# An encoder block on one core: value products of two heads side by side, low halves of seven weights made on DVE, and 20 instead of 16 k-tiles of the down projection in seven products

## Chip, core and metric

One core of one Trainium2 chip. The metric is the device time of one execution in microseconds (us). Of the kernel before there are three timed executions; one further execution was profiled.

## What is computed

One encoder block on 512 tokens of 1024 channels, batch 1, in float32. Two mixers work side by side on the normalised input, attention with 8 query heads and 2 key/value heads of 64, and a Mamba-2 state space model in both directions; gates merge them, an output projection and a residual follow, and then a SwiGLU feed-forward layer of width 2816.

```python
h = rms_norm(x, norm1_pre)
q, k, v, z, xbc, dt_raw, gates = split_cols(h @ w_in, IN_SPLITS)
attn_out = gqa_attention(rope(rms_norm(q)), rope(rms_norm(k)), v) @ w_attn_proj
ssd_out = ssd_branch(z, xbc, dt_raw, ...) @ w_ssd_proj
g_attn, g_ssd = split(sigmoid(gates), 2)
x = x + rms_norm((g_attn * attn_out + g_ssd * ssd_out) @ w_out, norm1_post)
gate, up = split(rms_norm(x, norm2_pre) @ w_gate_up, 2)
x = x + rms_norm((silu(gate) * up) @ w_down, norm2_post)
```

## The kernel before

**High and low halves.** To keep float32 accuracy, each operand of a large matmul is split in a high half (`whi`, a cast on ACT, L144) and a low half (`wlo`, the operand less its high half), and each product is three matmuls (`mm3`, L178 to L180, and `mm3f`, L1125). `weights()` lists the weights in the order of their use with a letter that says who makes the low half. "v" and "g" are a subtract on DVE or on POOL (L149). "d" is a negation on ACT (L146) and a DMA, issued by POOL, that reads the weight a second time and adds it in flight (L147). `presplit` carries this out, up to `AHEAD` weights before the use.

**Attention.** For each head the scores are made (L635, L636), a softmax follows, and `transpose_probs` turns the probabilities on PE (L653) with copies to SBUF by DVE and ACT. For each pair of heads eight value products of 64 columns of weights follow (L677): for each of four key tiles one product for either head, the one into the lower half of a PSUM bank, the other into the upper. A tile scheduler orders the instructions of this part; the z and gate products fill in between.

**Feed-forward.** `act` holds 22 k-tiles of 128 channels by 512 tokens. From the output projection on, PE's order is that of the program; the other engines' is the scheduler's.

**Down projection** (`down_start`, `down`). The output has four token tiles and two halves of 512 columns, in eight PSUM banks. The first 6 k-tiles are plain: 24 matmuls of 512 columns each. The other 16 (`PAIRS` = 8 pairs) are one 2 by 2 block product with a fast scheme of seven products: tokens split in halves `lo` and `hi`, k-tiles in two halves, columns in two halves. A pair of k-tiles takes 42 matmuls so. The seven products (into `u`, `v`, `a`, `x`, `u`, `a`, `y`) are each cut in groups of two k-tiles (`NG2` = 4 groups). `prep(g)` makes the high and low halves of a group's weights (`wsplit`, L1195 on ACT, L1196 on DVE) and activations (`asplit`, L1201, L1202), and `work(g)` issues the matmuls; `prep` stands one group ahead. Sums of blocks of weights are formed in `chain` (`ch`): once a group has been split, a DMA issued by POOL adds the next block into it (L1225). A second buffer `p3` holds the sum that the fourth product needs. Sums of activations are made by DVE behind the groups (`sums`, L1312 and L1313).

**Tail.** `begin(t)` squares the second column half of token tile `t` and multiplies it by the gain; `finish(t)` does so with the first half, makes the reciprocal root and writes the output with the residual (L1270). In the last product `last(2)` and `last(3)` do the sum and `finish` of the last two token tiles.

Of the kernel before, what the change touches and what calls it, by code (L numbers as in the profile page):

```python
# [14 lines left out]
ALU = mybir.AluOpType  # L15
# [4 lines left out]
P = 128  # L20
# [5 lines left out]
NQ = 8  # L26
# [18 lines left out]
PAIRS = 8  # L45
# [15 lines left out]
class Block:  # L61
# [41 lines left out]
    def weights(self):  # L103

        a = self.a
        for k0, kn in ((0, 3), (3, 3), (6, 2)):
            yield a["w_kv"][:, k0 : k0 + kn, :], kn * 288, "v" if k0 == 0 else "d"
        for j in range(12):
            yield a["w_xbc"][j], 1024, "g" if j < 3 else "d"
        for n in range(2):  # L110
            for i in range(4):
                yield a["w_z"][n, i], 1024, "gd"[n]
        for j in range(2 * KD):
            yield a["w_g"][j], 1024, "d"
# [533 lines left out]
    def transpose_probs(self, prs):  # L648
        pt = []
        for k in range(NT):  # L650
            pp = self.ps("sb")
            for t in range(NT):
                self.T.transpose(pp[:, t * P : t * P + P], prs[t][:, k * P : k * P + P], self.ident)  # L653
# [5 lines left out]
    def attention(self, decays):  # L659
# [3 lines left out]
        for h in range(NQ):  # L663
# [8 lines left out]
            if h % 2:  # L672
                po = self.ps("sc")
                for k in range(NT):
                    for i in range(2):
                        g = (h - 1 + i) // (NQ // NKV)
# [476 lines left out]
    def down(self, pool):  # L1153
# [7 lines left out]
        p3 = [new("p3", [2, 512], NG2) for _ in range(NG2)]  # L1161
# [9 lines left out]
        mm3, plain, bank = self.mm3f, self.plain, self.bank  # L1171

        for k in range(1, n0):
            if k > 1:
                self.down_operands(k, pool)
                if k < n0 - 2:
                    for t, n in bank:
                        plain(k, t, n)
            if k == 1:
                gain = [new("gn", [512], 2) for _ in range(2)]  # L1180
                for i in range(2):
                    self.load(gain[i], self.a["norm2_post"][i * 512 : i * 512 + 512].partition_broadcast(P))
            if k >= 2 and k - 2 < NG2:
                self.load(chain[k - 2], blk(k - 2, 0, 0))
        for t, n in reversed(bank):
            for k in (n0 - 2, n0 - 1):
                plain(k, t, n)
# [28 lines left out]
        def product(dst, b, a, start, after=None, sums=None, by_token=None, then=None):  # L1216
# [3 lines left out]
            def prep(g):  # L1220
# [3 lines left out]
                if after:  # L1224
                    G.dma_start(chain[g], after(g), accum_op=ALU.add)  # L1225

            def work(g):
                for k in (2 * g, 2 * g + 1):
                    x, wi = kept[k]
                    for t in range(1 if by_token else 2):  # L1230
                        mm3(dst[t], [y[:, t * P : t * P + P] for y in x], wi, start and k == 0)
                    if sums:
                        sums(k)
                if g == NG2 - 1:
                    if by_token:
                        by_token()
                        for x, wi in kept:
# [11 lines left out]
        def begin(t):  # L1249
# [5 lines left out]
            self.square_sum(ss[:, 0:1], c[t, 1], self.rstd[:, t : t + 1])  # L1255
            V.tensor_scalar(ss[:, 0:1], ss[:, 0:1], 1.0 / D, EPS, ALU.mult, ALU.add)
            V.tensor_tensor(c[t, 1], c[t, 1], gain[1], ALU.mult)
            half[t] = x, ss

        def finish(t):  # L1260
            x, ss = half[t]
            r2 = self.rstd[:, t : t + 1]
            self.square_sum(ss[:, 1:2], c[t, 0], r2)
            V.tensor_tensor(c[t, 0], c[t, 0], gain[0], ALU.mult)
# [4 lines left out]
            for i in (1, 0):  # L1269
# [8 lines left out]
        def third_weights():  # L1278
            for g in range(NG2):
                self.load(p3[g], blk(g, 0, 1))  # L1280
                G.dma_start(p3[g], blk(g, 1, 1), accum_op=ALU.add)
# [10 lines left out]

        def sums6():
            for t in range(2):
# [5 lines left out]
                begin(2 + t)  # L1300
# [5 lines left out]
        def last(t):  # L1306
            add(t, 0, y[t - 2])
            finish(t)

        between = {4: lambda: begin(0), 5: lambda: begin(1), 6: lambda: finish(0), 7: lambda: finish(1)}  # L1310
        product(u, lambda g: chain[g], a11, True, lambda g: blk(g, 0, 1),
                lambda k: V.tensor_tensor(r1[k], a22(k), a21(k), ALU.subtract), then=third_weights)  # L1312
        product(v, lambda g: raw(g, 1, 0), a12, False, None, lambda k: V.tensor_tensor(a21(k), a11(k), a21(k), ALU.subtract),  # L1313
                then=sums2)
        product(a, lambda g: chain[g], lambda k: r1[k], True, lambda g: blk(g, 1, 1),
                lambda k: V.scalar_tensor_tensor(r1[k], r1[k], -1.0, a11(k), ALU.mult, ALU.subtract), then=lambda: second(a))
        product(x, lambda g: p3[g], a21, True, None,
                lambda k: V.scalar_tensor_tensor(a12(k), r1[k], -1.0, a12(k), ALU.mult, ALU.subtract), then=lambda: second(x))
# [132 lines left out]
```

## Time and profile before

| what | us |
|---|---|
| three timed executions | 827.84, 830.14, 832.91 |
| median | 830.14 |
| profiled execution, own time | 830.12 |
| its span in the trace | 828.2 |
| mean granted clock of TensorE | 0.991 |

The profiled execution's time is 1.9 us longer than the span that the trace covers. In all views times count from the span's start. A row of the timeline gives start and duration of an instruction, or of several of one kind in a row (x2, x3). A duration includes the drain of the pipeline: of two instructions in a row the second starts before the end that is shown for the first. A piece of the chain of waits has start, length and what the time went to.

### The profile page before, as it was taken

Reading aid. Unit: us, or ns where it says so; the run is one execution under the profiler, and the core shown is the slowest. Engines: PE = TensorE matmul, PEld = TensorE weight load, DVE = VectorE, ACT = ScalarE, POOL = GpSimd, SP = SyncE. Lnnn points to the kernel's source line nnn. Section 1 sums busy time; section 2 is a strip of 40 time slices with the busy share of each in tenths; the row PEclk is TensorE's granted clock in tenths of the full one; section 3 lists DMA queues with packets and bytes.
Section 4 is the critical chain, followed back from the end, with each engine's and each line's share of the span. In section 5 each row is a group of like instructions: output and inputs, shape, how many; then the busy total and the mean of one; then the engine's idle time right before and its main releaser. Section 6 shows DMA issues by size and latency. Waiting matters only on the chain.

```text
span 828.2 us, 12209 instructions
## 1 busy us (share of the span) xinstructions
PE 804.9 (97%) x4522; PEld 676.8 (82%) x4522; DVE 578.4 (70%) x999; ACT 465.8 (56%) x841; POOL 200.0 (24%) x162
## 2 busy tenths in 40 slices
PE   8899999999899999999999999999999999999994
PEld 7688887666676777777888798999999999888883
DVE  3959785656335456685783799788888878837988
ACT  7767875745844442166333656555555555536673
POOL 3443430100132244539451002000000100041200
PEclk9999999999999999999999999999999999999998
DMA  9757830620875665137335453667766664899642
GB/s 314 218 134 159 200 93 27 140 64 1 216 176 130 158 150 124 52 114 252 116 129 185 164 153 91 188 193 188 193 177 185 182 178 140 286 288 245 104 93 102
DMA packets 49658, 130.52 MB, mean 158 GB/s; under 512 B 5568, under 2 KB 5952, under 8 KB 49600
## 3 DMA queue, kind: packets, MB, share of 16 engines
q1 hardware_dynamic: 38048, 95.46, 33.7%
q0 software_dynamic: 11552, 34.30, 24.0%
q8 instruction: 35, 0.57, 0.3%
q14 instruction: 23, 0.19, 0.1%
HBM read 121.35 MB, written 8.39 MB: 157 GB/s over the span
## 4 chain that ended last, share of the span: by engine, by line
PE 83%; DVE 5%; DMA 4%; ACT 3%; issue 2%; POOL 1%; SPq 1%; DVEq 0%; ACTq 0%; POOLq 0%
PE sa L972 10%; PE mm L178 8%; PE mm L179 8%; PE mm L180 8%; PE sc L972 7%; PE sb L1125 4%; PE sa L1125 4%; PE mm L972 3%; PE sb L972 3%; PE mm L1125 3%; PE sc L178 3%; PE sc L180 3%; PE sc L179 3%; PE sc L677 2%; PE sa L179 2%
## 5 line engine op out<-in xcount | busy, mean ns | idle before, releaser
L144 ACT CAST whi<-raw 128x1024 fp32r<-128x1024 f32 (+3 forms) x69 | 68.0, 992 | 20.6 <-PE sc L180 9.8
L178 PE MATMUL mm<-hT,wlo 128*128 128x512 f32 x176 | 73.8, 419 | 2.1 <-DMA wlo<-in_w_g 2.1
L149 POOL TENSOR_TENSOR wlo<-raw,whi 128x1024 fp32r<-128x1024 f32 (+1 forms) x28 | 58.2, 2081 | 65.5 <-ACT whi L144 63.9
L180 PE MATMUL mm<-hT,whi 128*128 128x512 f32 x176 | 69.7, 396 | 0.0
L179 PE MATMUL mm<-hT,whi 128*128 128x512 f32 x176 | 69.3, 394 | 0.0
L1023 POOL DMA_DIRECT2D raw<-in_w_gu x19 | 16.4, 861 | 211.5 <-ACT x L1114 54.8
L1028 ACT CAST whi<-raw 128x512 fp32r<-128x512 f32 (+1 forms) x57 | 41.6, 762 | 33.9 <-DMA raw<-in_w_gu 12.9
L1029 DVE TENSOR_TENSOR wlo<-raw,whi 128x512 fp32r<-128x512 f32 (+1 forms) x57 | 47.8, 866 | 16.3 <-ACT whi L1028 16.3
L972 PE MATMUL sa<-R,whi 128*128 128x256 f32 x304 | 56.4, 283 | 0.0
L972 PEld LDWEIGHTS sa<-R,whi 128*128 128x128 f32 x304 | 47.5, 192 | 0.0
L146 ACT ACTIVATE wlo<-raw 128x1024 fp32r<-128x1024 f32 (+2 forms) x31 | 32.3, 1043 | 26.4 <-PE mm L178 24.4
L972 PE MATMUL sa<-R,wlo 128*128 128x256 f32 x152 | 43.1, 283 | 0.0
L178 PEld LDWEIGHTS mm<-hT,wlo 128*128 128x128 f32 x176 | 33.3, 189 | 11.8 <-issue 3.2
L147 POOL DMA_DIRECT2D wlo<-in_w_g x16 | 13.8, 863 | 112.6 <-ACT wlo L146 66.7
L179 PEld LDWEIGHTS mm<-hT,whi 128*128 128x128 f32 x176 | 33.3, 189 | 8.7 <-issue 2.4
L180 PEld LDWEIGHTS mm<-hT,whi 128*128 128x128 f32 x176 | 33.3, 189 | 7.6 <-issue 0.5
L638 DVE TENSOR_REDUCE nmax<-sa 128x1 f32<-128x512 f32 x32 | 21.6, 686 | 19.9 <-PE sa L636 19.7
L972 PE MATMUL sa<-h2T,b 128*128 128x256 f32 x228 | 30.5, 283 | 0.0
L641 ACT ACTIVATE pr<-sa,nmax 128x512 f32<-128x512 f32 x32 | 22.0, 688 | 14.6 <-DVE rc L643 7.4
L972 PEld LDWEIGHTS sa<-R,wlo 128*128 128x128 f32 x152 | 29.2, 192 | 0.0
L155 ACT ACTIVATE junk<-z 128x512 bf16<-128x512 f32 x8 | 5.0, 628 | 42.6 <-DVE z L785 42.5
L972 PEld LDWEIGHTS sa<-h2T,b 128*128 128x128 f32 x228 | 28.7, 192 | 0.0
(475 smaller groups left out, 2552.8 us busy)
## 6 DMA issues: line engine op xcount, KB each, us to landing
raw<-in_w_gu SPq DMA_DIRECT2D x44, 512.0 KB, 4.7
raw<-in_w_gu POOLq DMA_DIRECT2D x19, 512.0 KB, 5.4
raw<-in_w_g SPq DMA_DIRECT2D x16, 512.0 KB, 6.0
wlo<-in_w_g POOLq DMA_DIRECT2D x16, 512.0 KB, 6.8
raw<-in_w_dn SPq DMA_DIRECT2D x14, 512.0 KB, 7.2
raw<-in_w_xbc SPq DMA_DIRECT2D x12, 512.0 KB, 4.9
ch<-in_w_dn POOLq DMA_DIRECT2D x12, 512.0 KB, 7.2
b<-in_w_gu SPq DMA_DIRECT2D x19, 256.0 KB, 5.8
```

The costliest lines, as they stand in the source:

```text
L144: self.A.copy(h[:, :n], raw[:, :n])
L146: self.A.mul(l[:, :n], raw[:, :n], -1.0)
L149: e.tensor_tensor(l[:, :n], raw[:, :n], h[:, :n].bitcast(F32), ALU.subtract)
L178: self.T.matmul(o, ll, rh, start=first, stop=False)
L179: self.T.matmul(o, lh, rl, start=False, stop=False)
L180: self.last_mm = self.T.matmul(o, lh, rh, start=False, stop=last)
L638: V.tensor_reduce(nmax, ps, AX.X, ALU.max, negate=True)
L641: self.last_exp = A.activation(pr, ps, AF.Exp, bias=nmax, accum_out=sm)
L972: self.T.matmul(dst, x, y[:, k], start=start and k == 0 and i == 0, stop=k == 3 and i == 2, skip_group_check=True)
L1028: A.copy(dst[0], src)
L1029: lo.tensor_tensor(dst[1], src, dst[0].bitcast(F32), ALU.subtract)
L1125: self.T.matmul(o, x, y, start=start and i == 0, stop=i == 2, skip_group_check=True)
```

## The change

Three parts. In `attention` the value products of a head pair are issued behind the last transpose of the second head, and listed as alternating heads. In `weights` the second key/value group, the second half of the z weights and the first two gate weights change their letter from "d" to "v". In `down` 20 of the 22 k-tiles go through the seven products (10 pairs, 5 groups), the two plain ones are those of `down_start`; `p3` goes. Instead blocks (0,0) and (0,1) are loaded into `b11` and `chain`. Behind a group's split in the first product POOL adds `chain` to `b11` (`first_sums`, L1275 of the changed program) and a DMA adds block (1,1) to `chain`; behind the fourth and fifth product further blocks are added to `chain`. The final normalisation can begin with either column half: token tiles 0 and 1 begin with half 0 behind the fourth product, 2 and 3 with half 1 behind the fifth, and 0 and 1 finish in the last product behind its k-tiles 8 and 9. Six of the eight gain products go to POOL. In the last product the first group serves both token tiles at once, and only the last four groups are split by token.

```diff
@@ -42,7 +42,7 @@
 R_DTB, R_AL, R_D, R_QK, R_END = 0, 32, 64, 80, 336
 
 
-PAIRS = 8
+PAIRS = 10
 NPLAIN = 3
 
 
@@ -104,14 +104,14 @@
 
         a = self.a
         for k0, kn in ((0, 3), (3, 3), (6, 2)):
-            yield a["w_kv"][:, k0 : k0 + kn, :], kn * 288, "v" if k0 == 0 else "d"
+            yield a["w_kv"][:, k0 : k0 + kn, :], kn * 288, "d" if k0 == 6 else "v"
         for j in range(12):
             yield a["w_xbc"][j], 1024, "g" if j < 3 else "d"
         for n in range(2):
             for i in range(4):
-                yield a["w_z"][n, i], 1024, "gd"[n]
+                yield a["w_z"][n, i], 1024, "gv"[n]
         for j in range(2 * KD):
-            yield a["w_g"][j], 1024, "d"
+            yield a["w_g"][j], 1024, "v" if j < 2 else "d"
         for j in range(KD):
             yield a["w_ap"][j], 512, "g"
         for j in range(KD):
@@ -650,7 +650,7 @@
         for k in range(NT):
             pp = self.ps("sb")
             for t in range(NT):
-                self.T.transpose(pp[:, t * P : t * P + P], prs[t][:, k * P : k * P + P], self.ident)
+                self.last_tr = self.T.transpose(pp[:, t * P : t * P + P], prs[t][:, k * P : k * P + P], self.ident)
             d = self.slot("t", [S], name="pt")
             (self.A.copy if k % 2 else self.V.tensor_copy)(d, pp)
             pt.append(d)
@@ -671,9 +671,10 @@
             yield 1.8
             if h % 2:
                 po = self.ps("sc")
-                for k in range(NT):
-                    for i in range(2):
-                        g = (h - 1 + i) // (NQ // NKV)
+
+                for k, i in ((k, i) for k in range(NT) for i in range(2)):
+                    g = (h - 1 + i) // (NQ // NKV)
+                    with self.tc.issue_after(self.last_tr.ins):
                         self.T.matmul(po[i * HD : i * HD + HD, :], self.vt[:, k, g * HD : g * HD + HD], pts[h - 1 + i][k],
                                       start=k == 0, stop=k == NT - 1)
                 hi, lo = self.slot("q", [S], F32R, "aTh"), self.slot("q", [S], F32R, "aTl")
@@ -1158,7 +1159,7 @@
         NG2 = PAIRS // 2
         new = lambda tag, shape, bufs, dt=F32: pool.tile([P] + shape, dt, tag=tag, name=self.nm(tag), bufs=bufs)
         chain = [new("ch", [2, 512], NG2) for _ in range(NG2)]
-        p3 = [new("p3", [2, 512], NG2) for _ in range(NG2)]
+        b11 = [new("b11", [2, 512], NG2) for _ in range(NG2)]
         r1 = [new("r1", [256], PAIRS) for _ in range(PAIRS)]
         splits = [new("as", [2, 256], 10, F32R) for _ in range(10)]
         cs = [new("c", [512], 8) for _ in range(8)]
@@ -1168,23 +1169,14 @@
             j = n0 + k * PAIRS + 2 * g
             return wd[j : j + 2, :, n * 512 : n * 512 + 512].rearrange("k p c -> p k c")
 
-        mm3, plain, bank = self.mm3f, self.plain, self.bank
-
-        for k in range(1, n0):
-            if k > 1:
-                self.down_operands(k, pool)
-                if k < n0 - 2:
-                    for t, n in bank:
-                        plain(k, t, n)
-            if k == 1:
-                gain = [new("gn", [512], 2) for _ in range(2)]
-                for i in range(2):
-                    self.load(gain[i], self.a["norm2_post"][i * 512 : i * 512 + 512].partition_broadcast(P))
-            if k >= 2 and k - 2 < NG2:
-                self.load(chain[k - 2], blk(k - 2, 0, 0))
-        for t, n in reversed(bank):
-            for k in (n0 - 2, n0 - 1):
-                plain(k, t, n)
+        mm3, bank = self.mm3f, self.bank
+
+        for g in range(NG2):
+            self.load(b11[g], blk(g, 0, 0))
+            self.load(chain[g], blk(g, 0, 1))
+        gain = [new("gn", [512], 2) for _ in range(2)]
+        for i in range(2):
+            self.load(gain[i], self.a["norm2_post"][i * 512 : i * 512 + 512].partition_broadcast(P))
         c = {(t, 1): cs.pop() for t in (2, 3, 0, 1)}
         for (t, n), x in c.items():
             A.copy(x, bank[t, n])
@@ -1222,19 +1214,19 @@
                 for i in range(2):
                     kept.append((asplit(a(2 * g + i)), [y[:, i * 512 : i * 512 + 512] for y in w]))
                 if after:
-                    G.dma_start(chain[g], after(g), accum_op=ALU.add)
+                    after(g)
 
             def work(g):
                 for k in (2 * g, 2 * g + 1):
                     x, wi = kept[k]
-                    for t in range(1 if by_token else 2):
+                    for t in range(1 if by_token and g >= NG2 - 4 else 2):
                         mm3(dst[t], [y[:, t * P : t * P + P] for y in x], wi, start and k == 0)
                     if sums:
                         sums(k)
                 if g == NG2 - 1:
                     if by_token:
                         by_token()
-                        for x, wi in kept:
+                        for x, wi in kept[2 * (NG2 - 4) :]:
                             mm3(dst[1], [y[:, P : 2 * P] for y in x], wi)
                     if then:
                         then()
@@ -1246,27 +1238,27 @@
 
         half = {}
 
-        def begin(t):
+        def begin(t, n):
 
             x = [new("x2", [512], 4) if t < 2 else self.slot("a", [512], name="x2") for _ in range(2)]
             for i in range(2):
                 self.load(x[i], self.x2_d[t][:, i * 512 : i * 512 + 512])
             ss = self.tiny(2, "ss")
-            self.square_sum(ss[:, 0:1], c[t, 1], self.rstd[:, t : t + 1])
+            self.square_sum(ss[:, 0:1], c[t, n], self.rstd[:, t : t + 1])
             V.tensor_scalar(ss[:, 0:1], ss[:, 0:1], 1.0 / D, EPS, ALU.mult, ALU.add)
-            V.tensor_tensor(c[t, 1], c[t, 1], gain[1], ALU.mult)
+            G.tensor_tensor(c[t, n], c[t, n], gain[n], ALU.mult)
             half[t] = x, ss
 
-        def finish(t):
+        def finish(t, n):
             x, ss = half[t]
             r2 = self.rstd[:, t : t + 1]
-            self.square_sum(ss[:, 1:2], c[t, 0], r2)
-            V.tensor_tensor(c[t, 0], c[t, 0], gain[0], ALU.mult)
+            self.square_sum(ss[:, 1:2], c[t, n], r2)
+            (G if t < 2 else V).tensor_tensor(c[t, n], c[t, n], gain[n], ALU.mult)
             v = self.tiny(1, "rv")
             V.tensor_scalar(v, ss[:, 1:2], 1.0 / D, ss[:, 0:1], ALU.mult, ALU.add)
             r = self.rsqrt(v, 1, True)
             V.tensor_tensor(r, r, r2, ALU.mult)
-            for i in (1, 0):
+            for i in (1 - n, n):
                 V.scalar_tensor_tensor(c[t, i], c[t, i], r, x[i], ALU.mult, ALU.add)
                 self.load(self.out[t * P : t * P + P, i * 512 : i * 512 + 512], c[t, i])
 
@@ -1275,10 +1267,13 @@
         x = [self.ps("sb") for _ in range(2)]
         v, y = [bank[t, 0] for t in (0, 1)], [bank[t, 0] for t in (2, 3)]
 
-        def third_weights():
-            for g in range(NG2):
-                self.load(p3[g], blk(g, 0, 1))
-                G.dma_start(p3[g], blk(g, 1, 1), accum_op=ALU.add)
+        def more(k, n):
+
+            return lambda g: G.dma_start(chain[g], blk(g, k, n), accum_op=ALU.add)
+
+        def first_sums(g):
+            G.tensor_tensor(b11[g], b11[g], chain[g], ALU.add)
+            more(1, 1)(g)
 
         def sums2():
             for t in range(2):
@@ -1289,6 +1284,11 @@
         def second(p):
             for t in range(2):
                 add(2 + t, 1, p[t], ALU.subtract)
+
+        def third():
+            second(x)
+            for t in range(2):
+                begin(t, 0)
 
         def sums6():
             for t in range(2):
@@ -1297,7 +1297,7 @@
                 add(2 + t, 1, u[t], ALU.subtract)
                 add(t, 1, u[t], ALU.subtract)
                 add(2 + t, 0, x[t])
-                begin(2 + t)
+                begin(2 + t, 1)
 
         def sums3():
             for t in range(2):
@@ -1305,18 +1305,18 @@
 
         def last(t):
             add(t, 0, y[t - 2])
-            finish(t)
-
-        between = {4: lambda: begin(0), 5: lambda: begin(1), 6: lambda: finish(0), 7: lambda: finish(1)}
-        product(u, lambda g: chain[g], a11, True, lambda g: blk(g, 0, 1),
-                lambda k: V.tensor_tensor(r1[k], a22(k), a21(k), ALU.subtract), then=third_weights)
+            finish(t, 0)
+
+        between = {8: lambda: finish(0, 1), 9: lambda: finish(1, 1)}
+        product(u, lambda g: b11[g], a11, True, first_sums,
+                lambda k: V.tensor_tensor(r1[k], a22(k), a21(k), ALU.subtract))
         product(v, lambda g: raw(g, 1, 0), a12, False, None, lambda k: V.tensor_tensor(a21(k), a11(k), a21(k), ALU.subtract),
                 then=sums2)
-        product(a, lambda g: chain[g], lambda k: r1[k], True, lambda g: blk(g, 1, 1),
+        product(a, lambda g: b11[g], lambda k: r1[k], True, None,
                 lambda k: V.scalar_tensor_tensor(r1[k], r1[k], -1.0, a11(k), ALU.mult, ALU.subtract), then=lambda: second(a))
-        product(x, lambda g: p3[g], a21, True, None,
-                lambda k: V.scalar_tensor_tensor(a12(k), r1[k], -1.0, a12(k), ALU.mult, ALU.subtract), then=lambda: second(x))
-        product(u, lambda g: chain[g], lambda k: r1[k], False, lambda g: blk(g, 1, 0), then=sums6)
+        product(x, lambda g: chain[g], a21, True, more(0, 0),
+                lambda k: V.scalar_tensor_tensor(a12(k), r1[k], -1.0, a12(k), ALU.mult, ALU.subtract), then=third)
+        product(u, lambda g: chain[g], lambda k: r1[k], False, more(1, 0), then=sums6)
         product(a, lambda g: raw(g, 1, 1), a12, False, then=sums3)
         product(y, lambda g: chain[g], a22, False, None, lambda k: between.get(k, int)(), lambda: last(2))
         stages[0][0]()
```

On PE, a pair of heads, before: `sb` is the bank of the second head's transposes, `sc` that of the value products, `pt` the turned probabilities, `mm` a z or gate product.

```order
L677 MATMUL sc_1618<-pt_1468,vt_448 64x512
L178 MATMUL mm_1605<-whi_1172,hT_344 128x512
L179 MATMUL mm_1605<-wlo_1173,hT_342 128x512
...
L653 MATMUL sb_1598<-cst_100,pr_1433 128x128
L653 MATMUL sb_1598<-cst_100,pr_1444 128x128
L677 MATMUL sc_1618<-pt_1582,vt_448 64x512
L677 MATMUL sc_1618<-pt_1475,vt_448 64x512
L677 MATMUL sc_1618<-pt_1589,vt_448 64x512
L677 MATMUL sc_1618<-pt_1482,vt_448 64x512
L677 MATMUL sc_1618<-pt_1596,vt_448 64x512
L677 MATMUL sc_1618<-pt_1489,vt_448 64x512
L677 MATMUL sc_1618<-pt_1603,vt_448 64x512
```

And now:

```order
L653 MATMUL sb_1597<-cst_100,pr_1421 128x128
L653 MATMUL sb_1597<-cst_100,pr_1432 128x128
L653 MATMUL sb_1597<-cst_100,pr_1443 128x128
L678 MATMUL sc_1617<-pt_1467,vt_447 64x512
L678 MATMUL sc_1617<-pt_1581,vt_447 64x512
L678 MATMUL sc_1617<-pt_1474,vt_447 64x512
L678 MATMUL sc_1617<-pt_1588,vt_447 64x512
L678 MATMUL sc_1617<-pt_1481,vt_447 64x512
L678 MATMUL sc_1617<-pt_1595,vt_447 64x512
L678 MATMUL sc_1617<-pt_1488,vt_447 64x512
L678 MATMUL sc_1617<-pt_1602,vt_447 64x512
L180 MATMUL mm_1604<-whi_1235,hT_342 128x512
```

The product that stood alone among the `mm` matmuls now stands with the other seven behind the transposes, in alternation of the heads.

On DVE, the key/value stage, before (`h` and `hT` are the normalised input and its low halves, `wlo` the low half of a key/value group):

```order
L149 TENSOR_TENSOR wlo_356<-raw_135,whi_355 128x864
L184 TENSOR_TENSOR hT_343<-h_351,hT_341 128x512
L184 TENSOR_TENSOR hT_343<-h_359,hT_341 128x512
L294 SCALAR_TENSOR_TENSOR h_368<-xT_110,gcol_99,rbs_349 128x512
L294 SCALAR_TENSOR_TENSOR h_372<-xT_115,gcol_99,rbs_349 128x512
L294 SCALAR_TENSOR_TENSOR h_381<-xT_120,gcol_99,rbs_349 128x512
L184 TENSOR_TENSOR hT_343<-h_368,hT_341 128x512
```

The same place now:

```order
L149 TENSOR_TENSOR wlo_356<-raw_135,whi_355 128x864
L184 TENSOR_TENSOR hT_343<-h_351,hT_341 128x512
L184 TENSOR_TENSOR hT_343<-h_359,hT_341 128x512
L149 TENSOR_TENSOR wlo_364<-raw_137,whi_363 128x864
L294 SCALAR_TENSOR_TENSOR h_367<-xT_110,gcol_99,rbs_349 128x512
L294 SCALAR_TENSOR_TENSOR h_371<-xT_115,gcol_99,rbs_349 128x512
L294 SCALAR_TENSOR_TENSOR h_380<-xT_120,gcol_99,rbs_349 128x512
```

A second subtract of 128 by 864 stands ahead of the `h` and `hT` of the later k-tiles.

On DVE, in the first product of the down projection, now (`as` is a split activation, `r` and `act` the sums of activations):

```order
L1312 TENSOR_TENSOR r_1526_7374<-act_6670,act_5330 128x256
L1312 TENSOR_TENSOR r_1527_7375<-act_4342,act_5464 128x256
L1188 TENSOR_TENSOR wlo_7423<-b_1517_7365,whi_7422 128x1024
L1194 TENSOR_TENSOR as_7388<-act_5866,as_7388 128x256
L1194 TENSOR_TENSOR as_7389<-act_6000,as_7389 128x256
L1312 TENSOR_TENSOR r_1528_7376<-act_4343,act_5598 128x256
L1312 TENSOR_TENSOR r_1529_7377<-act_4344,act_5732 128x256
L1312 TENSOR_TENSOR r_1530_7378<-act_4345,act_5866 128x256
L1312 TENSOR_TENSOR r_1531_7379<-act_4346,act_6000 128x256
L1188 TENSOR_TENSOR wlo_7433<-b_1518_7366,whi_7432 128x1024
L1313 TENSOR_TENSOR act_4737<-act_4737 128x256
L1313 TENSOR_TENSOR act_4928<-act_4928 128x256
```

and on POOL, from the last weight load of the layer ahead on:

```order
L1024 DMA raw_7130<-in_w_gu 128x1024
L1275 TENSOR_TENSOR b_1517_7365<-b_1517_7365,ch_7360 128x1024
L1272 DMA ch_7360<-in_w_dn 128x2x512
L1275 TENSOR_TENSOR b_1518_7366<-b_1518_7366,ch_7361 128x1024
L1272 DMA ch_7361<-in_w_dn 128x2x512
...
L1275 TENSOR_TENSOR b_1521_7369<-b_1521_7369,ch_7364 128x1024
L1272 DMA ch_7364<-in_w_dn 128x2x512
L1249 TENSOR_TENSOR c_7393<-c_7393,gn_7408 128x512
L1249 TENSOR_TENSOR c_7392<-c_7392,gn_7408 128x512
L1272 DMA ch_7360<-in_w_dn 128x2x512
```

Each subtract `wlo<-b` on DVE is now followed on POOL by a sum into the same `b` and a DMA into `ch`, and behind the fifth stand gain products (L1249). The sums and the gain products on POOL are new; DMAs into `ch` stood there before too.

## Rows read from the trace of the kernel before

**Rows 1.** The page, busy times of the engines (share of the span, instructions)

```profile
PE 804.9 (97%) x4522; PEld 676.8 (82%) x4522; DVE 578.4 (70%) x999; ACT 465.8 (56%) x841; POOL 200.0 (24%) x162
```

**Rows 2.** Waits of PE by releaser: us in total, times, longest

```profile
PE sb L179 <- DMA wlo<-in_w_kv: 3.3, 1, 3.3
PE mm L178 <- DMA wlo<-in_w_g: 2.1, 1, 2.1
PE mm L179 <- DMA wlo<-in_w_z: 1.8, 2, 1.3
```

**Rows 3.** Chain of waits, key/value stage: start us, us, what

```profile
29.83 8.72 DMA wlo<-in_w_kv
...
42.40 0.24 PE sb L180
...
43.10 0.14 PE sa L178
```

**Rows 4.** Chain of waits, first gate weights

```profile
213.71 0.43 PE mm L179
```

**Rows 5.** Windows: us, busy times (x instructions), PEclk (granted clock), DMA share, GB/s

```profile
40.00:45.00 5.00, 5.00 (x30) 5.00 (x30) 2.87 (x6) 3.83 (x7) 2.41 (x1) 0.73 0.19 73
210.00:220.00 10.00, 7.92 (x36) 6.33 (x35) 5.36 (x14) 6.53 (x13) 0.86 (x1) 0.83 1.05 281
```

**Rows 6.** Chain of waits, value products (two records each) of two head pairs

```profile
179.14 3.58 PE sc L677 x16
...
223.18 1.00 PE sc L677 x2
...
225.20 3.58 PE sc L677 x14
```

**Rows 7.** Chain of waits, down projection

```profile
718.99 1.36 PE sc L1125 x6
...
740.75 10.88 PE sa L1125 x48
```

**Rows 8.** Timeline of DVE and POOL, key/value stage and around the first product

```profile
29.83 2.06 DVE L294 SCALAR_TENSOR_TENSOR h<-xT,gcol,rbs 128x512 f32<-128x512 f32 x3
...
33.62 4.21 DVE L294 SCALAR_TENSOR_TENSOR h<-xT,gcol,rbs 128x512 f32<-128x512 f32 x3
37.76 1.88 DVE L184 TENSOR_TENSOR hT<-h,hT 128x512 fp32r<-128x512 f32 x3
...
33.58 2.38 POOL L149 TENSOR_TENSOR wlo<-raw,whi 128x1024 fp32r<-128x1024 f32 x1 [1.82 <-ACT whi L144]
...
710.34 0.69 DVE L1055 SCALAR_TENSOR_TENSOR act<-up,g 128x512 f32<-128x512 f32 x1
...
714.56 0.76 DVE L1202 TENSOR_TENSOR as<-act,as 128x256 fp32r<-128x256 f32 x2
...
719.59 2.36 DVE L149 TENSOR_TENSOR wlo<-raw,whi 128x1024 fp32r<-128x1024 f32 x2
```

**Rows 9.** Groups of instructions, POOL and DVE: busy us, mean ns; L862: ns min/median/max

```profile
L149 POOL TENSOR_TENSOR wlo<-raw,whi 128x1024 fp32r<-128x1024 f32 x20 | 47.9, 2396 | 49.3 <-ACT whi L144 47.7 <-issue 1.6
...
L859 POOL TENSOR_TENSOR at<-at,ga 128x512 f32<-128x512 f32 x8 | 10.8, 1350 | 6.5 <-ACT at L693 6.4
...
L862 DVE TENSOR_TENSOR gs<-gs,at x8: 676/2545/2904, 402.3 to 433.4; 128x512 f32<-128x512 f32 x8
```

**Rows 10.** Timeline of the end, PE and DVE

```profile
817.34 0.39 PE L1125 MATMUL sc<-whi,as 128*128 128x512 f32 x1
...
815.85 2.73 DVE L1270 SCALAR_TENSOR_TENSOR c<-c,ry,x 128x512 f32<-128x512 f32 x4
...
823.48 1.41 DVE L1270 SCALAR_TENSOR_TENSOR c<-c,ry,x 128x512 f32<-128x512 f32 x2
```

**Rows 11.** DMA issues of 742 to 746 and 759 to 800: median us to landing

```profile
ch<-in_w_dn POOLq DMA_DIRECT2D x2, 512.0 KB, 17.6
...
ch<-in_w_dn POOLq DMA_DIRECT2D x8, 512.0 KB, 6.2
```

## Prediction

> **What bounds the kernel.** I read the engines' busy shares first: PE is busy in 97% of the span, so only three things can change the time: work that PE loses, waits of PE, and what runs behind its last matmul [rows 1]. Then the waits of PE: three stand out, and all three end with a low half of a weight that a DMA delivers [rows 2]. The chain of waits shows two of them as single pieces and, behind each, matmuls at twice their usual pitch [rows 3, 4]; the windows show the granted clock falling in the same places [rows 5]. The chain also gives the price of the value products [rows 6] and of the down projection's matmuls [rows 7]. Where the change loads DVE and POOL, I read their own rows [rows 8, 9]; the end of the trace gives the tail [rows 10], and the DMA issues give the landing of POOL's accumulates [rows 11].
>
> **Where the sum starts.** The profiled execution took 830.12 us, 0.02 below the median of three runs (830.14). A measurement of this kernel tells some 0.5% (4.15 us) from no change, so faster means below 826.0 and slower above 834.3.
>
> **Part 1, value products.** The chain has 8 products side by side (16 records) in 3.58 us. A pair of heads whose first product stands alone pays 1.00 for that one and again 3.58 for the other seven [rows 6]. Three of the four head pairs are of that kind, the fourth already has all eight together; in the new order all four have. The transposes and their copies stay. −3 × 1.00 = **−3.0**.
>
> **Part 2, key/value weights.** The second k-group's low half changes from ACT's negation plus POOL's accumulate DMA to a subtract on DVE. The DMA took 8.72 from issue to landing and PE waited 3.3 of it; then 13 matmuls, the last at 42.40, ran 0.24 apart instead of 0.13, which is 1.4 more [rows 2, 3], in a window whose granted clock was 0.73 [rows 5]. Some of those 4.7 will be lost again: the new subtract costs DVE about 1.1 (a subtract of 1024 columns takes 1.14 in a run of two) and stands ahead of the `h` and `hT` operations that PE needs next, which ended at 39.64 [rows 8]. With weights there in time PE reaches the last `hT` tiles while DVE still makes them; I take a new wait of 1.2. **−3.5**, bounds −2 and −4.7. The third group keeps its DMA.
>
> **Part 3, z weights.** Four low halves change in the same way; PE's two waits on them, 1.8, go [rows 2]: **−1.8**, bounds 0 and −1.8.
>
> **Part 4, the first two gate weights.** The wait of 2.1 goes [rows 2], and so do the seven matmuls behind it at 0.43 instead of 0.227, with a step of 0.31 behind them (1.5) [rows 4, 7], where the granted clock was 0.83 [rows 5]: **−3.6**, bounds −2 and −3.6. The third weight still comes by DMA and has the first two weights' products to land under. Parts 3 and 4 put six subtracts of some 1.2 on DVE between 150 and 215, where ACT is freed of six negations. DVE is busy in 70% of the span [rows 1], so I charge nothing; if it were on the path there, six times 1.2, 7 us, would be the most.
>
> **Part 5, fewer matmuls.** 48 matmuls take 10.88, so one takes 0.2267 [rows 7]. A plain k-tile is 24 matmuls, a pair of k-tiles in seven products 42. Four tiles move: −96 + 84 = −12 matmuls, **−2.7**.
>
> **Part 6, the first product.** Before, eight banks of plain tiles stood between the second plain tile (its end is where the third begins, 718.99) and the first product [rows 7]. Now the product begins there. Each of its five groups is 12 matmuls, 12 × 0.2267 = 2.72, so the fifth group's weights are due at 719.0 + 4 × 2.72 = 729.9. DVE is free for this at 710.95 and has, in its new order, 35 operations of 256 columns (0.335 each, from pairs 0.67 apart) and five subtracts of 1024 (1.14) to do up to the fifth one [rows 8]: 11.7 + 5.7 = 17.4, done at 728.4. That fits, with 1.5 to spare.
>
> But POOL now adds `ch` to `b11` five times, once behind each of DVE's subtracts, on the same 1024 columns that take it 2.40 [rows 9]. The trace shows what such an instruction does to DVE. Three `h` operations took 2.06 alone and 4.21 with a POOL subtract beside them [rows 8]: 2.15 of POOL's 2.38 are lost to DVE. A product of 512 columns with both inputs in SBUF (L862), beside which POOL worked too, has a least time of 0.68 and a median of 2.5 [rows 9]. Nearly all that DVE does in the first product has both inputs in SBUF. Four sums stand ahead of the fifth subtract: 4 × 2.15 = 8.6, done at 737.0, **7.1** late. PE's wait comes in pieces at groups two to five; for the longest I add **1.5** of slower clock, as behind the waits in parts 2 and 4. Together +8.6; bounds 0, if POOL's sums fall where DVE idles, and 10.
>
> The Trainium skill ("SBUF — State Buffer", section "Who interferes with whom") says that a DVE instruction with two SBUF inputs contends with a GpSimd instruction that reads SBUF, and that the second to issue is blocked fully until the first ends. By that rule each sum would cost DVE its whole 2.40, the product would be 8.1 late and the total 1.0 higher; the trace agrees in kind and shows a little less, 2.15 of 2.38 [rows 8].
>
> **Part 7, the last product.** Two gain products move from DVE to POOL right behind DVE's sums of tokens 2 and 3, ahead of DVE's splits for the last product. On POOL a 512-wide product takes 1.35 [rows 9], so up to 2.7 of DVE is blocked; its lead over PE there is small, since these splits stand one group ahead of their use and behind eight operations on sums. I take **+2.3** and **+1.5** of clock; bounds 0 and 4.2. The other four gain products on POOL lie beside products for which DVE has time.
>
> **Part 8, the tail.** PE's last matmul ended at 817.73 and DVE's last output at 824.89, 7.2 later [rows 10]. In between DVE finished outputs of tokens 0 and 1 until 818.58, 0.85 past PE's end, and wrote token 2's two outputs, 1.41, ahead of token 3's gain product [rows 10]. Both now lie before PE's end, but for a small rest: **−2.0**, bounds −0.8 and −2.3.
>
> The new loads (ten of 512 KB) go out where before's chain loads did; the first product needs two per 2.72, and the ones it needs first are queued first. I charge nothing; their cover is the two plain tiles ahead of the product, 48 matmuls or 10.9, and without it PE would wait in the first product for loads in place of sums.
>
> **Sum.** −3.0 − 3.5 − 1.8 − 3.6 = −11.9 ahead of the down projection; −2.7 + 8.6 + 3.8 − 2.0 = +7.7 in it. Total −4.2: 830.12 − 4.2 = **825.9**.
>
> **Rivals.**
>
> *POOL's sums do not hold DVE up* (they find its idle time, or DVE has the lead that I deny it). Then the down projection gives −2.7 − 2.0 and the change is −11.9 − 4.7 = −16.6: **813.5**. For it: without POOL, DVE just fits. Against it: [rows 8, 9] show the hold wherever the two meet, and the slack is 1.5.
>
> *The chain's accumulate lands late: slower.* In the fourth product POOL adds block (0,0) into `ch` by DMA, and the very next product uses it; before, a whole product lay between. From DVE's subtract to the next use are one product, 13.6, less the group that the split runs ahead, 2.72, and POOL's issue, 1.2: 9.7. An accumulate of this kind landed 6.2 after its issue late in the stage, 17.6 in the crowded stretch [rows 11]. The point from which it decides is 9.7; at 17.6 PE waits 7.9 and then 1.5 of clock: 825.9 + 9.4 = **835.3**. Against it: the crowd in that stretch was of token loads and weights together, and less is in flight there now.
>
> *The waits removed upstream come back* (on `hT`, on the next weight by DMA, on DVE's queue): only some 5 of the 11.9 are gained, 830.12 − 5 + 7.7 = **832.8**. For it: DVE gets seven more subtracts in stages where PE needs DVE's other results. Against it: PE's long waits there ended with DMAs, not with DVE [rows 2].
>
> **Chances and range.** Forecast case 0.55, POOL harmless 0.18, waits come back 0.15, late accumulate 0.12. The forecast's own bounds reach from about 821 to 831, with slightly over half of it below 826.0: faster 0.18 + 0.30 = 0.48; slower 0.12 + 0.02 = 0.14; same 0.38. The range takes in the first rival and the third and leaves out the second: **813 to 834**; the forecast case alone 821 to 831.
>
> **What would show it.** Right: no wait on `wlo` by DMA in the kv, z and first gate stages; four runs of eight value products of 3.58; POOL rows of 2.4 behind each of DVE's subtracts in the first product, and DVE rows of two or three times their length beside them; PE waiting there for `wlo` or `as` by some 6 to 8 in total; DVE ending about 5 behind PE. Wrong: DVE rows at 0.34 and 1.14 beside POOL's sums (then 813), a PE wait on `ch` by DMA at the fifth product (then 835), or a new wait for `hT` in the kv stage as long as the old one.

## The result, and the profile after

The changed kernel takes 834.96 us (median of 14 runs), the kernel before 830.73 (14 runs on the same chips): a ratio of 1.0051, 95% interval 1.0036 to 1.0067. It is 4.2 us slower where 4.2 less were forecast, 1 us above the range. The profiled execution took 836.36, its span is 834.5 us, 6.3 longer than before's.

The waits of PE after the change, the longest of the whole span (us in total, times, longest), answer to [rows 2]:

```profile
PE sa L1126 <- DVE wlo L1188: 8.0, 3, 7.3
PE sa L1126 <- ACT whi L1187: 2.8, 1, 2.8
PE mm L1126 <- DVE wlo L1188: 2.7, 1, 2.7
...
PE sb L178 <- DVE hT L184: 0.9, 1, 0.9
```

The three waits on DMAs are gone, at the price of 0.9 on `hT`. All the long ones are now in the down projection (L1126). The chain's value products answer to [rows 6]; four pairs, none with a product that stands alone:

```profile
151.65 3.58 PE sc L678 x16
...
213.01 3.58 PE sc L678 x16
```

So the part ahead came out as forecast: the first plain tile starts at 694.24 instead of 706.46, 12.2 earlier. Everything was lost behind it. From the second plain tile's end PE needed 117.15 us (706.60 to 823.75) for what took 98.90 before (718.83 to 817.73). The timeline of PE shows where; the rows that open a stall in the first, fifth (two) and sixth product (two):

```profile
722.79 0.79 PE L1126 MATMUL sa<-wlo,as 128*128 128x512 f32 x1 [7.34 <-DVE wlo L1188]
...
773.80 0.80 PE L1126 MATMUL sa<-whi,as 128*128 128x512 f32 x1 [2.77 <-ACT whi L1187]
775.06 0.80 PE L1126 MATMUL sa<-wlo,as 128*128 128x512 f32 x1 [0.46 <-DVE wlo L1188]
...
799.75 0.50 PE L1126 MATMUL mm<-whi,as 128*128 128x512 f32 x1 [0.33 <-ACT whi L1187]
802.98 0.50 PE L1126 MATMUL mm<-wlo,as 128*128 128x512 f32 x1 [2.73 <-DVE wlo L1188]
```

An undisturbed product is 60 matmuls, 13.6. From the first matmul of one product to that of the next they took 23.4, 13.65, 13.6, 16.55, 17.3, 18.85 and, to the end of the last matmul, 13.8. That is 9.8 too much in the first, 6.65 in the fourth and fifth together, and 5.25 in the sixth. The 6.65 belong to the fifth product's weights: the wait of 2.77 stands ahead of its first matmul and so counts with the fourth. More than the waits is lost, since the granted clock is lower in the stretches around them, 0.71 and 0.73 in these two windows (columns as in [rows 5]):

```profile
720.00:730.00 10.00, 7.05 (x24) 5.41 (x25) 10.00 (x7) 2.07 (x4) 9.05 (x5) 0.71 0.85 142
...
774.00:786.00 12.00, 11.54 (x38) 8.89 (x39) 9.90 (x16) 7.86 (x15) 4.78 (x4) 0.73 1.12 201
```

**The first product.** The timeline of POOL and DVE there:

```profile
704.77 9.10 POOL L1275 TENSOR_TENSOR b<-b,ch 128x1024 f32<-128x1024 f32 x1 [31.69 <-DVE wlo L1188]
...
714.95 2.82 POOL L1275 TENSOR_TENSOR b<-b,ch 128x1024 f32<-128x1024 f32 x1
...
718.85 2.79 POOL L1275 TENSOR_TENSOR b<-b,ch 128x1024 f32<-128x1024 f32 x1
...
706.57 1.22 DVE L1188 TENSOR_TENSOR wlo<-b,whi 128x1024 fp32r<-128x1024 f32 x1
...
710.05 1.22 DVE L1188 TENSOR_TENSOR wlo<-b,whi 128x1024 fp32r<-128x1024 f32 x1
711.18 2.96 DVE L1194 TENSOR_TENSOR as<-act,as 128x256 fp32r<-128x256 f32 x2
714.07 4.33 DVE L1313 TENSOR_TENSOR act<-act 128x256 f32<-128x256 f32 x3
718.32 4.42 DVE L1188 TENSOR_TENSOR wlo<-b,whi 128x1024 fp32r<-128x1024 f32 x1
722.66 3.18 DVE L1194 TENSOR_TENSOR as<-act,as 128x256 fp32r<-128x256 f32 x2
```

The hold works in both directions. POOL's first sum shows 9.10 where such an instruction takes 2.40 [rows 9]: for nearly its first 7 us, some fifteen instructions, DVE runs at full pace, a subtract in 1.22. Then POOL is in, and DVE is the one that stands: two splits of 0.34 take 2.96, three sums of 0.34 take 4.33, a subtract of 1.14 takes 4.42. Three of POOL's sums lie beside these. PE's 7.3 end with that subtract; it makes the low half that the fourth group needs.

**The fifth product.** POOL's queue around the fourth:

```profile
750.51 16.53 POOL L1249 TENSOR_TENSOR c<-c,gn 128x512 f32<-128x512 f32 x2 [18.30 <-ACT junk L155]
766.98 6.16 POOL L1272 DMA_DIRECT2D ch<-in_w_dn  x5
```

and DVE, at the first and the last subtract of the fourth product's weights before 763 and at the sums from PSUM behind:

```profile
755.37 1.22 DVE L1188 TENSOR_TENSOR wlo<-ch,whi 128x1024 fp32r<-128x1024 f32 x1
...
761.00 1.22 DVE L1188 TENSOR_TENSOR wlo<-ch,whi 128x1024 fp32r<-128x1024 f32 x1
762.13 1.28 DVE L1237 TENSOR_TENSOR c<-c,mm 128x512 f32<-128x512 f32 x2
```

Two gain products took 16.5, where a product of that size takes 1.35 on POOL [rows 9], while DVE worked without a gap on operations with both inputs in SBUF. The first ended only as DVE came to `c` sums, which read PSUM. Behind them in POOL's queue stand the five accumulates into `ch` that the fifth product needs. The first could have gone at 756.6, when its buffer had been split; it went at 767.0.

**The tail.** PE's last matmul ends at 823.75, DVE's last output at 830.89: 7.1 later, as before [rows 10]. Two more gain products on POOL took 5.1 there and ended at 818.0. On DVE the four outputs of tokens 0 and 1, the sum of token 2 and its two outputs:

```profile
818.28 2.74 DVE L1262 SCALAR_TENSOR_TENSOR c<-c,ry,x 128x512 f32<-128x512 f32 x4
820.94 0.68 DVE L1237 TENSOR_TENSOR c<-c,sc 128x512 f32<-128x512 f32 x1
...
824.55 1.42 DVE L1262 SCALAR_TENSOR_TENSOR c<-c,ry,x 128x512 f32<-128x512 f32 x2
```

The outputs of tokens 0 and 1 are done before PE's end, as forecast. But the sum of token 2, whose last matmul ended at 818.3, stood behind them until 820.94, and token 2's outputs still come after PE's end.

### The profile page after: what moved, and what is told of

It reads as the page before. It is cut to its first block, busy times and chain, and to the rows that moved or that the text cites. A ratio compares the mean times of both kernels' runs of the same rounds, so it can differ in the third digit from the quotient of the medians.

```text
span 834.5 us, 12236 instructions
## 1 busy us (share of the span) xinstructions
PE 802.9 (96%) x4510; PEld 675.0 (81%) x4510; DVE 608.2 (73%) x1021; ACT 462.4 (55%) x847; POOL 236.9 (28%) x165
## 4 chain that ended last, share of the span: by engine, by line
PE 70%; DVE 12%; DMA 7%; issue 4%; ACT 4%; POOL 2%; DVEq 0%; SPq 0%; ACTq 0%; POOLq 0%
PE sa L973 9%; PE mm L180 8%; PE mm L178 8%; PE mm L179 8%; PE sc L973 6%; DVE wlo L1188 3%; PE sb L973 3%; PE mm L973 3%; PE sc L178 3%; PE sc L180 3%; PE sc L179 3%; DMA raw<-in_w_dn 2%; PE sc L678 2%; PE sb L653 2%; DMA ch<-in_w_dn 2%
## 5 line engine op out<-in xcount | busy, mean ns | idle before, releaser
L144 ACT CAST whi<-raw 128x1024 fp32r<-128x1024 f32 (+3 forms) x65 | 63.9, 989 | 17.8 <-PE sc L180 12.3
L147 POOL DMA_DIRECT2D wlo<-in_w_g x14 | 12.1, 863 | 141.6 <-PE mm L179 78.6
L146 ACT ACTIVATE wlo<-raw 128x1024 fp32r<-128x1024 f32 (+1 forms) x24 | 25.1, 1048 | 24.3 <-PE mm L178 24.2
L1126 PE MATMUL sa<-whi,as 128*128 128x512 f32 x80 | 28.3, 432 | 2.8 <-ACT whi L1187 2.8
L1275 POOL TENSOR_TENSOR b<-b,ch 128x1024 f32<-128x1024 f32 x5 | 20.7, 4146 | 32.1 <-DVE wlo L1188 32.1
L767 DVE COPY_PREDICATED sa<-cst,sa 128x512 f32<-128x512 uint32 x16 | 11.1, 693 | 24.6 <-PE sa L764 24.6
```

Source lines behind the costliest of these rows:

```text
L144: self.A.copy(h[:, :n], raw[:, :n])
L146: self.A.mul(l[:, :n], raw[:, :n], -1.0)
L1126: self.T.matmul(o, x, y, start=start and i == 0, stop=i == 2, skip_group_check=True)
L1275: G.tensor_tensor(b11[g], b11[g], chain[g], ALU.add)
```

## The experiments

Eleven kernels ran, each beside the kernel before on the same chip. "Product" means the time from its first matmul to that of the next, in the profiled execution. Where a run is set against the changed kernel, which ran on other chips, each is taken by its distance to the kernel before on its own chip; the changed kernel's is +4.2.

**1. The parts ahead of the down projection alone.** The diff's hunks in `weights`, `transpose_probs` and `attention`, on the kernel before.

> The kernel before with the two parts ahead of the down projection only (value products side by side, seven low halves on DVE); the down projection stays as it was. Theory: these parts give their whole 12.2 us and the down projection of the change alone cost 18.3, so this kernel takes 830.7 - 12.2 = 818.5 us. Rival: part of the 12 us is given back later, since the feed-forward's weights and DVE's queue are no further along; then 822 us or more.

Measured: 815.74 us against 829.62, ratio 0.983 (0.981 to 0.985). The parts ahead give 13.9, more than the 12.2 expected. The gain is not given back, and the two halves of the change pull in opposite directions.

**2. The down projection's part alone.** The other hunks, on the kernel before.

> The kernel before with the down projection's part of the change alone. Theory (the parts do not touch each other): 829.5 plus 19 (835.0 less the 815.7 of the other parts alone), 848 to 849. Rival (part of the loss comes from the parts ahead, which bring the first product's loads closer to the feed-forward's): 845 or less.

Measured: 846.48 against 829.42, ratio 1.021 (1.017 to 1.025): 17.1 slower, between the two expectations; the changed kernel and experiment 1 together ask for 4.2 + 13.9 = 18.1. The same products are long: 23.4 the first, 32.0 instead of 27.2 the fourth and fifth together, 19.0 the sixth. The loss is the down projection's own, but for up to some 4 us that the interval (13.8 to 21.0 slower) leaves open.

**3. Value products alone.**

> The kernel before with the value products of a pair side by side, and nothing else. Theory: three products of 1.00 us that stood alone go: 3.0 us less than before (829.6), 826.6, and the seven low halves give the other 10 to 11 of the 13.9 us that both gave together. Rival (the value products were hidden behind other waits): no change.

Measured: 827.13 against 829.45, ratio 0.997 (0.9955 to 0.998), 1.7 to 3.7 less: the 3.0 lie inside. In the profiled execution, 1.3 above the median, PE reached the down projection only 1.0 earlier, since PE's waits on the three groups of DMAs took 9.0 in all instead of 7.2 [rows 2]. The low halves give the other 11 or so.

**4. POOL's sums replaced by accumulate DMAs.**

```diff
-            G.tensor_tensor(b11[g], b11[g], chain[g], ALU.add)
+            G.dma_start(b11[g], blk(g, 0, 1), accum_op=ALU.add)
```

> The changed kernel with POOL's five sums into b11 replaced by five more accumulate DMAs that read block (0,1) again. Theory (POOL's sums and DVE's splits hold each other up, and that is what PE waited for in the first product, 7.3 us and the slow clock behind it, 9.8 us over the product's 13.6): the product takes 13.6 to 14.5 and the total falls from 835.0 to 825 to 826. Rival (the loads of the first product come late, POOL's sums are beside the point): no change, or slower by 1 to 3, since 2.6 MB more are moved in a stretch where the DMA engines are busy all the time.

Measured: 837.83, ratio 1.010 (1.007 to 1.013). Both were half right. DVE is not held any more: its last subtract of the first product waits for ACT, and that for a load. But the transfers crowd; the DMA issues of 690 to 740 (median us to landing), where the changed kernel has 6.2 for `raw` and 5.7 for the accumulates into `ch`:

```profile
raw<-in_w_dn SPq DMA_DIRECT2D x6, 512.0 KB, 13.4
...
ch<-in_w_dn POOLq DMA_DIRECT2D x5, 512.0 KB, 19.7
b<-in_w_dn POOLq DMA_DIRECT2D x5, 512.0 KB, 20.6
```

The first product falls to 19.3, and the second rises from 13.65 to 21.1. So a cure by DMA does not by itself separate POOL's hold from the loads; the next experiment does.

**5. POOL's sums made by DVE.**

```diff
-            G.tensor_tensor(b11[g], b11[g], chain[g], ALU.add)
+            V.tensor_tensor(b11[g], b11[g], chain[g], ALU.add)
```

> The changed kernel with the five sums into b11 made by DVE instead of POOL; loads and DMAs as in the changed kernel, and the scheduler sets DVE's order anew. Theory (DVE loses its time in the first product to POOL's sums, not to their work and not to loads): DVE has five more instructions of 1.14, 5.7 us, but nothing holds it; the wait of 7.3 shrinks to 3 or less and the product from 23.4 to 14 to 18, total 826 to 830. Rival (late loads, as in the version with DMAs only): the product stays above 20 and the total above 833.

Measured: 833.17, ratio 1.0045 (1.0025 to 1.0065). The first product came out as the theory has it, the total as the rival. The product takes 13.9 instead of 23.4, with five more instructions on DVE, the same loads and the same five DMAs issued by POOL: it was the hold by POOL's sums, not work and not loads. Most of the 9.5 is given back: the second product takes 18.1, the fourth and fifth 37.4 instead of 33.85, the last 15.4; only the sixth gains, 16.4 instead of 18.85. With DVE ahead of its work, POOL's gain products find still less room:

```profile
743.24 20.69 POOL L1249 TENSOR_TENSOR c<-c,gn 128x512 f32<-128x512 f32 x2 [23.05 <-ACT junk L155]
763.87 6.17 POOL L1272 DMA_DIRECT2D ch<-in_w_dn  x5
```

**6. All gain products on DVE.** `G` becomes `V` in `begin` and `finish`.

> The changed kernel with all eight gain products on DVE. Theory (two gain products on POOL, held up by DVE for 16.5 us, stand ahead of the accumulate DMAs that the fifth product's weights need): the DMAs go out some 10 us earlier, PE's wait of 3.2 at the start of the fifth product and the slow clock behind it go, about 6 us in all, and the outputs of tokens 0 and 1 come before PE's last matmul, 1 to 2 more: 827 to 829. Rival (the DMAs are late because they land late, 13.5 us in a crowded stretch): the wait stays within 1 us of 3.2 and the total is 833 to 836.

Measured: 825.27, ratio 0.995 (0.993 to 0.997), 8.6 less than the changed kernel (9.7 by the two medians as they stand). The fourth and fifth product take 27.2, no wait left; the sixth falls to 15.6, of which 2.0 are still too much, and the tail from 7.1 to 6.5.

**7. The gain products behind the accumulates.** Experiment 6 changes both who multiplies and who stands in POOL's queue. Here the products stay on POOL; in `begin` they are issued after the last accumulate that has been traced.

```diff
-            G.tensor_tensor(c[t, n], c[t, n], gain[n], ALU.mult)
+            with self.tc.issue_after(self.last_more.ins):
+                G.tensor_tensor(c[t, n], c[t, n], gain[n], ALU.mult)
```

> The changed kernel with the two gain products of tokens 0 and 1 still on POOL, but placed in its queue behind the five accumulate DMAs of the fourth product and one of the fifth. Theory (the fifth product's 6.5 us are the place in the queue: POOL's products, held up by DVE, stand ahead of the DMAs): the fifth product takes 13.6 to 14.5 as with the gains on DVE, the rest as in the changed kernel, total 828 to 830. Rival (it is DVE's time that POOL's products take): the fifth product stays above 17 and the total at 833 or more.

Measured: 825.59, ratio 0.995 (0.993 to 0.997), as with the products on DVE. POOL's queue:

```profile
754.98 1.20 POOL L1274 DMA_DIRECT2D ch<-in_w_dn  x1 [24.48 <-DVE wlo L1188]
...
768.09 11.00 POOL L1250 TENSOR_TENSOR c<-c,gn 128x512 f32<-128x512 f32 x2
```

The products still take 11.0, but the accumulates leave from 755.0, and products four to six take 13.6 each (the profiled execution, 822.79, is the fastest of the ten). It is the place in the queue. The sixth product is cured here too. That its loss followed from the fifth's alone is not shown: in experiment 6 the fifth was as clean, and 2.0 of the sixth's 5.25 stayed.

**8. The sixth product's weights loaded early.**

```diff
-        product(a, lambda g: raw(g, 1, 1), a12, False, then=sums3)
+        product(a, lambda g: b11[g], a12, False, then=sums3)
-        product(a, lambda g: b11[g], lambda k: r1[k], True, None,
+        product(a, lambda g: b11[g], lambda k: r1[k], True, lambda g: self.load(b11[g], blk(g, 1, 1)),
```

> The changed kernel with the sixth product's weights loaded into the five b11 buffers, each as soon as the third product has split what was there, in place of the raw buffers, of which the last two groups must wait. Theory (the sixth product's 5.3 us are a late load: the fourth group's load went out at 787.6 and took 10.9): they go, 829.5 to 831. Rival (it is ACT's and DVE's order, with the squares of tokens 2 and 3 ahead of the splits, that makes them late): within 1 us of 835.

Measured: 828.81, ratio 0.999 (0.998 to 1.000), 5.0 less than the changed kernel (6.2 by the medians as they stand). The sixth product takes 13.6, and 1.75 are gained in the fourth and fifth. So what made the sixth late was a load into one of three `raw` buffers (out at 787.6, landed 10.9 later). With experiments 6 and 7: the same load took 8.9 where accumulates still moved beside it, and 3.5 where POOL's gain products held the next accumulates back until it was out. So accumulates that move beside it make it late, most of all the delayed ones.

**9. Experiments 6 and 8 together.**

> The changed kernel with both cures together, gain products on DVE and the sixth product's weights loaded early; POOL's sums stay. Alone they gave 9.7 and 6.2 on 835. Theory (two causes; each also eased the other's place, since a late fifth product pushes loads and accumulates together): products two to seven all take 13.6 to 13.9 and the total is 822.5 to 824. Rival (one cause, the crowd of DMAs in products four to six, cured by either): 825, as with the gains alone.

Measured: 822.98, ratio 0.992 (0.990 to 0.994). The first product is left, 23.4; the second takes 14.3, all others 13.6, and the tail 5.7.

**10. As 9, with the sums by accumulate DMAs, and those into `ch` moved to the second product.**

> As the kernel with both cures, and the sums into b11 are made by accumulate DMAs; the loads of block (0,1) into ch and the accumulates onto them, which the fourth product needs, move from the first to the second product. Theory (in the version with DMAs only it was the crowd of 15 further transfers in the first product that made loads late): first product 13.6 to 15, all others 13.6 to 14, total 811 to 814. Rival (accumulate DMAs issued by POOL land after some 20 us whatever else is moved): waits at the third and fourth product, total 820 or more.

Measured: 817.17, ratio 0.985 (0.983 to 0.987), above the 811 to 814 expected. First product 14.2, second 16.95, third 14.1. The loads into `ch` did not move: nothing holds them back, and the scheduler put them right behind `b11`'s. The second product's fourth weight, in a `raw` buffer that came free at 714.6, is late.

**11. As 10, with that weight and the fifth in the two `ch` buffers that are free at the start.**

> As the version with sums by spread accumulates, and the second product's last two weights are loaded into the two ch buffers that are free, at the start, in place of raw buffers that come free late. Theory (the second product's 3.4 us too much are that load, out at 714.6 and landed 11 later): second product 13.6 to 14.2, total 813 to 814.5, below the 815.7 of the version with the parts ahead of the down projection only, as 12 fewer matmuls (2.7) ask. Rival (the accumulates crowd the third product's weights next): 816 or more.

Measured: 814.38 (813.97 to 815.61), ratio 0.982 (0.979 to 0.986): the lowest median of all, some 15 us below the kernel before. Waits of PE in the whole down projection:

```profile
PE sa L1126 <- ACT c L1183: 0.3, 1, 0.3
PE sb L1126 <- DVE wlo L1189: 0.2, 1, 0.2
```

It has the 20 k-tiles in products and beats both kernels. Against experiment 1 (815.74 on another chip) its interval overlaps: that the 12 matmuls now pay is not shown.

## Why the forecast failed, point by point

- **Parts 1 to 4, −11.9: right.** PE reached the down projection 12.2 earlier in the profile (13.5 in experiment 1's). The 1.2 taken for a new wait on `hT` measured 0.9. The value products' 3.0 and the low halves' remainder fit experiments 1 and 3.
- **Part 5, −2.7: right** as counted: an undisturbed product of 60 matmuls takes 13.6. That it shows in the total of any kernel here is open (experiment 11).
- **Part 6, +8.6: right** in the cause, and in size partly by luck. The first product measured 9.8 too much, and experiment 5 shows that POOL's hold on DVE is the cause. The form differs: DVE's loss comes late and in blocks, since POOL itself stood for nearly 7 us first, and PE's wait is one piece at the fourth group. Four sums of 2.15 each were counted up to the fifth subtract; three cost DVE 2.2, 3.2 and 3.2 up to the end of the fourth (2.96, 4.33 and 4.42 for what takes 0.75, 1.09 and 1.22 undisturbed), also 8.6. By the Trainium skill ("SBUF — State Buffer", section "Who interferes with whom"), where the second to issue is blocked fully, the term was 9.6, nearer to the 9.8; but its rule alone would not have POOL wait through some fifteen of DVE's instructions.
- **Part 7 is the step that failed.** It said: "The other four gain products on POOL lie beside products for which DVE has time." They cost DVE little, but they stood for 16.5 us at the head of POOL's queue with the fifth product's accumulates behind them. I had counted a hold in one direction, DVE's, and not the queue behind POOL's. That is 6.65 ahead of and in the fifth product, which experiments 6 and 7 take away, and part of the 5.25 in the sixth, whose load landed late among the delayed accumulates; the prediction had no term for that load. The +3.8 that I had placed in the last product is not there: that product took 13.8, no more than its 60 matmuls and the end of the last one (0.2) take.
- **Part 8, −2.0: wrong,** 0.0. The outputs of tokens 0 and 1 did come before PE's end, but so late that token 2's sum stood behind them, and its outputs came after PE's end as before. With the gain products on DVE 0.6 to 1.4 come (experiments 6 and 9).
- **The slower rival** had the right place (the accumulate between fourth and fifth product, 9.7 us of room) and the wrong reason. The DMAs did not land late, they left late: 10.4 behind the split; the first landed after 5.6. That its 835.3 lies so near the measured 834.96 is luck: it priced the wait at 9.4, kept the +3.8 and −2.0 that did not come, and had no loss in the sixth product.

The profiled sum: −12.2 − 2.7 + 9.8 + 6.65 + 5.25 = +6.8, against a span 6.3 longer; the rest is mainly 0.8 that the kernel before lost in its last product. The profiled execution is 1.4 above its kernel's median and before's 0.6 below; that is the distance to the 4.2 of the medians.

## What to carry to other kernels

Where a step moves to an engine with a queue of its own, ask who stands behind it there, and what it takes beside its neighbour's load, not alone: 1.35 became 8.3, the mean of two. An accumulate DMA issued by POOL is only as early as the POOL work ahead of it. A stall cured in one product moved to the next as long as loads and buffers had no slack (experiments 4 and 5), so the gain came when loads, sums and queue order were cured together.

## What the runs showed of the hardware that I had not expected

A POOL instruction with inputs in SBUF does not get in at DVE's next instruction boundary. With DVE issuing two-input operations without a gap, one of 128x512 stood 12.9 us instead of 1.35 (the longer of the two above) and two of them 20.7 in experiment 5; the first ended as DVE came to operations with an input in PSUM. In experiments 5 and 7 the first of the two likewise ended with such sums, at 756.5 and 771.8; the second in 7 ended only at 779.1, 1.2 after DVE had run out of work. The group of these instructions (ns min/median/max):

```profile
L1249 POOL TENSOR_TENSOR c<-c,gn x4: 1268/2514/12867, 750.5 to 802.8; 128x512 f32<-128x512 f32 x4
```

And accumulates of 512 KB issued by POOL landed after 5.7 us (median) in the changed kernel's first products and after 20 in experiment 4, where five more of them moved in the same stretch.
